# One-hots of a product-key gate build: token-by-token layout in place of lane-by-lane

## The chip, the cores and the metric

The kernel runs on one core of one Trainium2 chip. The metric is the device time of one execution in microseconds (us). The engines are named as in the profile: PE is TensorE (PEld its weight loads), DVE is VectorE, ACT is ScalarE, POOL is GpSimd, SP is SyncE, which only starts transfers here.

## The reference

One layer works on 256 tokens of width 2048: a retention group beside a gated recurrent group, then cross-attention to 256 memory tokens, then the part that matters here, a feed-forward of 16384 single-neuron experts (PEER):

```python
vals, ids = lax.top_k(sub_scores, 16)                    # 8 heads, two halves of 128 keys
cand = vals[:, :, 0, :, None] + vals[:, :, 1, None, :]
top_sc, pos = lax.top_k(cand.reshape(t, 8, 256), 16)     # 16 experts a head, 128 a token
eid = (i1 * 128 + i2).reshape(t, 128)
gate = jax.nn.softmax(top_sc, axis=-1).reshape(t, 128)
...
act = jax.nn.gelu(jnp.einsum('td,tkd->tk', xb, u_tab[eid]))
out = jnp.einsum('tk,tkd->td', gate * act, v_tab[eid])
```

A final RMSNorm follows. Everything is float32 at the interface.

## The kernel before

The 16384 experts are kept as 128 "rotated" rows of 128 lanes: a lane is a first index i1, and row r holds in lane i1 the expert whose second index is (r - i1) mod 128. The first 40 rows (`RD`) are computed densely, the other 88 (`RS`) only where tokens picked them: in each lane the 32 most used of them as dense columns as well, the rest by gathering single rows of U and V from HBM. The counts that decide this, and the gates of all rows, come out of the gate build.

A program order is written by hand as a main line of matmul blocks and a side line, `wv` (class `Weave`), a queue of generators. Each block of the main line calls `wv.pump(rate)`, which runs the side generators until their yields have used up that credit. The side code's instructions thus fall between those of the main line. Outside the stretches marked `manual_schedule`, the framework's planner may still change the order on each engine; data dependences are turned into semaphores by the framework.

The main line in the stretch at hand is `u_chunk` and `u_block` (L1173, L149): one column of U (128 experts) is two halves; each half is a load `raw<-in_U_dram` on SP's queue, a rounded copy `hi` on ACT (L135), the remainder `lo` on DVE (L136) and 24 matmuls (L156). The side line is `route`, which finds the 16 experts of each head, and then `gbuild` (L1116), which builds the gates.

`finish` (L830), called by `route` once for each half of 128 tokens, transposes the first index, the row number and the gate, so that a partition is a slot (8 heads times 16 picks) and a column is a token: `i1T`, `rT` in bfloat16, `gtT` in float32. It also fills a constant, `four` (L855): the numbers 0 to 127, each four times in a row, in bfloat16.

`gbuild` goes through the 256 tokens by four, 64 steps in all. A step does:

- two comparisons on DVE (L1132), which give `o2` (one-hot of the row number) and `c1` (one-hot of the first index), bfloat16, 128 partitions by 512 elements, laid out lane by lane: the four tokens of lane 0, the four of lane 1 and so on;
- a product on POOL (L1133): `og` is `o2` times the gate, float32, laid out token by token. It reads `o2` with a step of four elements;
- a copy on ACT (L1135): `o1` is `c1` in float32, token by token, read with the same step;
- one step later on PE: for each token a float32 product of `o1` and `og` (L1146) into the tile `G`, and a bfloat16 product of `c1` and the last 88 lanes of `o2` (L1149) that adds up counts in `cnt`. Both of its operands are read with a step of four elements;
- two copies on ACT (L1152, L1153) of `G` into the tiles `gs`.

The four arrays stand in rings of three (`n % 3`) within the tiles `kept`. Every eighth step ACT's queue issues three writes of `gs` to HBM (L1156, L1158, L1159, to `gd` and `gt`), and DVE multiplies two chunks of activations (L1164). When the counts are complete, `choose` (L956) picks the dense columns; `look_up` (L992), `compact` and the gathers (L1455, L1231) follow, and the main line goes on with U and then V.

Of the kernel before, what the change touches and what calls it, by code (L numbers as in the profile page):

```python
# [11 lines left out]
BF16 = mybir.dt.bfloat16  # L12
# [3 lines left out]
ALU = mybir.AluOpType  # L16
AX = mybir.AxisListType

P = 128
# [24 lines left out]
RD = 40  # L44
RS = P - RD
# [42 lines left out]
def hybrid_layer_kernel(ctx: ExitStack, tc: tile.TileContext, a: dict, out: bass.AP, dbg=None):  # L88
    nc = tc.nc
    V, A, G, PE = nc.vector, nc.scalar, nc.gpsimd, nc.tensor  # L90
# [28 lines left out]
    def sm(name):  # L119
        return ps2_.tile([P, 512], F32, tag="sm", name=name)  # L120

    ident = cp.tile([P, P], F32, name="ident")
    iota = cp.tile([P, P], F32, name="iota")
# [369 lines left out]
    for i in range(3):  # L493
        t = slot("qs" if i == 0 else "ms", [P, TT, 1024], "qkv"[i])
# [318 lines left out]
    i1T, rT, gtT, key, work, sel, sel2, idx = ({} for _ in range(8))  # L813
    flag = cp.tile([P, TT], F32, name="flag")

    def route():
# [11 lines left out]
        v4 = vals.rearrange("p (h c) j -> p h c j", c=2)  # L828
        i4 = idf.rearrange("p (h c) j -> p h c j", c=2)
        def finish(tt):  # L830
            four = gx["b"][:, 1536:1792].bitcast(BF16).rearrange("p (a b) -> p a b", b=4)
            gs = r3[:, 5, 0, :8]
            V.tensor_reduce(gs, gt, axis=AX.X, op=ALU.add)
            V.reciprocal(gs, gs)
            V.tensor_tensor(gt, gt, gs[:, :, None].to_broadcast([P, 8, 16]), op=ALU.mult)
            while "pb" not in done:
                yield 3.0
            i1, i2 = (ii[:, c].rearrange("p h j -> p (h j)") for c in range(2))
            rr = pgt.tile([P, P], F32, tag="rr", name="rr")
            tmp = tp.tile([P, P], F32, tag="gj", name="gj")  # L840
            V.tensor_tensor(rr, i1, i2, op=ALU.add)
            V.tensor_scalar(tmp, rr, float(P), -float(P), op0=ALU.is_ge, op1=ALU.mult)
            V.tensor_tensor(rr, rr, tmp, op=ALU.add)
            for _ in range(3):
                yield 2.0
            pt = sm("rT")
            for j, src in enumerate((i1, rr, gt.rearrange("p h j -> p (h j)"))):
                PE.transpose(pt[:, j * P:(j + 1) * P], src, ident)
            trio = gx["d"][:, 1536 + 256 * tt:1792 + 256 * tt]
            both = trio[:, :P].bitcast(BF16).rearrange("p (a b) -> p a b", a=2)  # L850
            A.copy(both, pt[:, :2 * P].rearrange("p (a b) -> p a b", a=2))
            A.copy(trio[:, P:], pt[:, 2 * P:3 * P])
            i1T[tt], rT[tt], gtT[tt] = both[:, 0], both[:, 1], trio[:, P:]
            if tt == 0:
                V.tensor_copy(four, iota[:, :, None].to_broadcast([P, P, 4]))  # L855
            nc.sync.dma_start(i1d[tt], both[:, 0])
            ri, rw = bits[tt], tmp
            V.tensor_copy(ri.bitcast(I32), rr)
            V.tensor_scalar(rw.bitcast(U32), ri, 3, None, op0=ALU.logical_shift_right)
            V.tensor_scalar(ri, ri, 7, None, op0=ALU.bitwise_and)  # L860
            V.tensor_copy(rw, rw.bitcast(I32))
            yield 1.0
            V.tensor_tensor(which[tt], iota[:, None, NCH:NCH + NW].to_broadcast([P, P, NW]),
                            rw[:, :, None].to_broadcast([P, P, NW]), op=ALU.is_equal)
            yield 1.3
            key[tt] = pgt.tile([P, P], F32, tag=f"key{tt}", name="key")
            work[tt] = pgt.tile([P, P], F32, tag=f"work{tt}", name="work")
            if tt == 0:
                jb = gx["b"][:, 1792:1920]
                V.tensor_scalar(tmp, iota, 1.0, None, op0=ALU.add)  # L870
                V.tensor_copy(jb.bitcast(I32), tmp)
                V.tensor_scalar(jb.bitcast(U32), jb.bitcast(U32), 23, None, op0=ALU.logical_shift_left)
                box["jb"] = jb
            V.tensor_scalar(rr, rr, float(P), -float(RD * P), op0=ALU.mult, op1=ALU.add)
            V.tensor_tensor(rr, rr, i1, op=ALU.add)
            V.tensor_copy(rr.bitcast(I32), rr)
            e, lead = rr.bitcast(U32), key[tt].bitcast(U32)
            gb, tu = gt.rearrange("p h j -> p (h j)").bitcast(U32), tmp.bitcast(U32)
            V.tensor_scalar(lead, e, 31, 31, op0=ALU.logical_shift_right, op1=ALU.logical_shift_left)
            V.tensor_tensor(lead, lead, box["jb"].bitcast(U32), op=ALU.bitwise_or)  # L880
            yield 1.5
            V.tensor_scalar(tu, gb, LOW, None, op0=ALU.bitwise_and)
            V.tensor_tensor(work[tt].bitcast(U32), tu, lead, op=ALU.bitwise_or)
            V.tensor_scalar(tu, e, 7, 1 << 20, op0=ALU.logical_shift_left, op1=ALU.bitwise_and)
            V.tensor_tensor(work[tt].bitcast(U32), work[tt].bitcast(U32), tu, op=ALU.bitwise_or)
            V.tensor_scalar(tu, gb, 20, 13, op0=ALU.logical_shift_right, op1=ALU.logical_shift_left)
            V.tensor_tensor(lead, lead, tu, op=ALU.bitwise_or)
            V.tensor_scalar(e, e, ROW, None, op0=ALU.bitwise_and)
            V.tensor_tensor(lead, lead, e, op=ALU.bitwise_or)
            yield 2.0  # L890
# [219 lines left out]
    acts, held_in, gx, bits, which, cnt = ({} for _ in range(6))  # L1110
# [5 lines left out]
    def gbuild():  # L1116
        prev = None
        cnt["t"] = pcn.tile([P, 512], F32, tag="cnt", name="cnt")
        rows = gt_.rearrange("(r p) t -> p r t", p=P)
        for n in range(T // 4 + 1):  # L1120
            nxt = None
            tt, t0 = divmod(4 * n, P)
            ss = slice(t0, t0 + 4)
            if n < T // 4:
                h0, q0 = n % 3 * 512, n % 3 * 256
                four = gx["b"][:, 1536:1792].bitcast(BF16).rearrange("p (a b) -> p a b", b=4)
                o1 = gx["a"][:, h0:h0 + 512].rearrange("p (a b) -> p a b", a=4)
                c1, o2 = (gx["d"][:, k + q0:k + q0 + 256].bitcast(BF16).rearrange("p (a b) -> p a b", b=4)
                          for k in (0, 768))
                og = gx["b"][:, h0:h0 + 512].rearrange("p (a b) -> p a b", a=4)  # L1130
                for o, ix in ((o2, rT), (c1, i1T)):
                    V.tensor_tensor(o, four, ix[tt][:, None, ss].to_broadcast([P, P, 4]), op=ALU.is_equal)  # L1132
                G.tensor_tensor(og, o2.rearrange("p a b -> p b a"), gtT[tt][:, ss, None].to_broadcast([P, 4, P]),  # L1133
                                op=ALU.mult)
                A.copy(o1, c1.rearrange("p a b -> p b a"))  # L1135
                nxt = (o1, o2, og, c1)
                yield 1.3
            if prev:
                o1, o2, og, c1 = prev
                m = n - 1  # L1140
                k = m % (GT // 4)
                if k == 0:
                    ga, gb = (slot(tag, [P, P // 2, GT], "gs") for tag in ("qs", "ms"))
                pt = sm("G")
                for j in range(4):
                    PE.matmul(pt.rearrange("p (c t) -> p c t", t=4)[:, :, j], o1[:, j], og[:, j],  # L1146
                              start=True, stop=True)
                for j in range(4):
                    PE.matmul(cnt["t"][:, :RS], c1[:, :, j], o2[:, RD:, j], start=(m == 0 and j == 0),  # L1149
                              stop=(m == T // 4 - 1 and j == 3))  # L1150
                ks = slice(4 * k, 4 * k + 4)
                A.copy(ga[:, :, ks], pt[:, :T].rearrange("p (c t) -> p c t", t=4))  # L1152
                A.copy(gb[:, :, ks], pt[:, T:].rearrange("p (c t) -> p c t", t=4))  # L1153
                if k == GT // 4 - 1:
                    ts = slice(4 * m + 4 - GT, 4 * m + 4)
                    A.dma_start(gd[:, :, m // (GT // 4)].rearrange("q p c t -> p q c t"),  # L1156
                                ga[:, 8 * ND:RD].rearrange("p (q c) t -> p q c t", c=8))
                    A.dma_start(rows[:, :P // 2 - RD, ts], ga[:, RD:])  # L1158
                    A.dma_start(rows[:, P // 2 - RD:, ts], gb)  # L1159
                    for i in range(ND):  # L1160
                        while f"u{i}" not in done:
                            yield 3.0
                        av = acts[i][:, :, ts]
                        V.tensor_tensor(av, ga[:, 8 * i:8 * i + 8], av, op=ALU.mult)  # L1164
                        yield 0.3
                yield 0.3
            prev = nxt
        done.add("gbuild")
# [717 lines left out]
```

## Time and profile before

| What | Value |
|---|---|
| Runs shown: median (lowest to highest) | 1977.03 us (1976.32 to 1978.99), 3 runs |
| Profiled execution, its own time | 1978.82 us |
| Its span, first to last instruction | 1977.0 us |
| Mean granted TensorE clock | 0.982 |
| Busy share of the span | PE 96%, PEld 80%, DVE 76%, ACT 43%, POOL 26% |
| First and last start of L1132 | 971.5 us and 1156.6 us |
| L1132, DVE, 128 instructions | 63.1 us busy |
| L1133, POOL, 64 instructions | 72.0 us busy |
| L1135, ACT, 64 instructions | 43.4 us busy |
| L1149, PE, 256 matmuls | 29.3 us busy |

Times in the views are microseconds from the start of the span, durations in group rows nanoseconds where they say "mean ns" or "duration ns". In a row of the timeline the first number is the start, the second the length, "x3" means that three instructions are merged, and the bracket gives the idle time before them and what ended it. The chain is followed back from the last instruction: at each step to what released it, or to its engine's instruction before.

### The profile page before, as it was taken

The page shows a single profiled execution, that of the slowest core. Times are in us where ns is not written, and L with a number is a line of the kernel's source. Part 1 is how long each engine was busy: PE and PEld are TensorE (multiplying, and loading weights), DVE is VectorE, ACT ScalarE, POOL GpSimd, SP SyncE. Part 2 cuts the span into 40 slices and gives each one's busy share as a digit, 9 for nine tenths or more (in the row PEclk, how much of TensorE's full clock was granted, in tenths as well). Part 3 has the DMA queues.
Part 4 walks back from the last instruction along what each step waited for, and adds up shares of the span by engine and source line. Part 5 has one row for each costly group of instructions (what it writes and reads, how often), then busy time and mean ns, then how long its engine had stood idle before and what let it go on. Part 6 is the DMA issues. An engine that isn't in the chain of part 4 may idle for free.

```text
span 1977.0 us, 28501 instructions
## 1 busy us (share of the span) xinstructions
PE 1896.1 (96%) x10644; PEld 1589.4 (80%) x10644; DVE 1500.9 (76%) x2304; ACT 851.6 (43%) x1324; POOL 517.7 (26%) x370
## 2 busy tenths in 40 slices
PE   9999999999999999999999887999989989999997
PEld 8888888888889888899899877988978668656563
DVE  6867968654566656899986667798879889687857
ACT  6566444544455554554456542333334343121111
POOL 0200010000000000000025421355443578477723
PEclk9999999999999999999999988999989999999999
DMA  8775755566664456755557888699898989999993
GB/s 297 260 224 170 208 195 182 154 185 195 185 185 156 149 167 217 251 176 164 186 179 142 166 258 277 235 395 362 321 383 318 383 315 399 379 387 372 421 411 125
DMA packets 203391, 500.97 MB, mean 253 GB/s; under 512 B 106777, under 2 KB 113049, under 8 KB 174873
## 3 DMA queue, kind: packets, MB, share of 16 engines
q1 hardware_dynamic: 72576, 256.33, 39.7%
q0 software_dynamic: 36096, 227.24, 29.5%
q10 hardware_dynamic: 94576, 15.54, 4.8%
q8 instruction: 84, 1.38, 0.3%
q14 instruction: 59, 0.48, 0.1%
HBM read 504.29 MB, written 21.30 MB: 266 GB/s over the span
## 4 chain that ended last, share of the span: by engine, by line
PE 56%; DMA 17%; DVE 14%; issue 9%; POOL 2%; ACT 2%; ACTq 0%; SPq 0%; POOLq 0%; DVEq 0%
PE wb L145 8%; PE xc L198 7%; PE xc L199 7%; PE xc L201 7%; DMA at<-in_Us_dram,idx 6%; PE acc L1213 6%; PE wb L147 4%; PE U L156 4%; DVE lo L136 4%; DMA gt<-gs 3%; DMA at<-in_Vs_dram,idx 2%; DMA kept<-in_V_dram 2%; PE G L1146 2%; PE acc L1194 2%; PE acc L1191 2%
## 5 line engine op out<-in xcount | busy, mean ns | idle before, releaser
L136 DVE TENSOR_TENSOR lo<-raw,hi 128x1024 fp32r<-128x1024 f32 x364 | 448.9, 1235 | 217.3 <-PE xc L201 125.7
L135 ACT CAST hi<-raw 128x1024 fp32r<-128x1024 f32 x364 | 382.1, 1053 | 352.4 <-PE xc L199 173.4
L156 PE MATMUL U<-xn,hi 128*128 128x256 f32 x1280 | 179.9, 292 | 3.8 <-ACT hi L135 3.8
L156 PEld LDWEIGHTS U<-xn,hi 128*128 128x128 f32 x1280 | 167.0, 199 | 4.7 <-ACT hi L135 4.7
L1462 DVE SCALAR_TENSOR_TENSOR junk<-at,h 128x2048 bf16<-128x2048 f32 x64 | 146.2, 2284 | 9.1 <-DMA at<-in_Us_dram,idx 8.9
L1470 DVE SCALAR_TENSOR_TENSOR hh<-at,coef,hh 128x2048 f32<-128x2048 f32 x46 | 108.0, 2348 | 47.3 <-DMA at<-in_Vs_dram,idx 46.7
L145 PE MATMUL U<-xn,hi 128*128 128x512 f32 x512 | 140.2, 407 | 0.0
L794 POOL DMA_DIRECT2D hn<-h x2 | 1.1, 565 | 510.4 <-DVE h L792 510.4
L1383 ACT CAST hi<-kept 128x1024 fp32r<-128x1024 f32 x52 | 53.6, 1051 | 186.9 <-DMA kept<-in_Vs_dram,dyn 127.0
L1455 POOL DMA_INDIRECT at<-in_Us_dram,idx x72 | 86.3, 1199 | 143.4 <-DVE junk L1462 114.4
L145 PE MATMUL wb<-hT,hi 128*128 128x512 f32 x448 | 116.9, 396 | 0.7 <-ACT hi L135 0.7
L1213 PE MATMUL acc<-kept,kept 128*128 128x512 f32 x256 | 110.2, 592 | 0.0
L1133 POOL TENSOR_TENSOR kept<-kept 128x512 f32<-128x512 bf16 x64 | 72.0, 1133 | 130.1 <-DVE kept L1132 90.2
L145 PEld LDWEIGHTS U<-xn,hi 128*128 128x128 f32 x512 | 92.9, 192 | 15.4
L156 PE MATMUL U<-xn,lo 128*128 128x256 f32 x640 | 96.0, 295 | 5.9 <-DVE lo L136 5.5
L1213 PEld LDWEIGHTS acc<-kept,kept 128*128 128x128 f32 x256 | 48.6, 190 | 60.4 <-issue 60.3
L156 PEld LDWEIGHTS U<-xn,lo 128*128 128x128 f32 x640 | 86.5, 201 | 9.2 <-DVE lo L136 8.9
L145 PEld LDWEIGHTS wb<-hT,hi 128*128 128x128 f32 x448 | 80.6, 189 | 14.8 <-ACT hi L135 0.9
L1400 DVE TENSOR_TENSOR lo<-uT,hi 128x512 fp32r<-128x512 f32 x128 | 81.8, 682 | 11.6 <-ACT hi L1381 8.7
L145 PE MATMUL wb<-xT,hi 128*128 128x512 f32 x352 | 90.1, 398 | 0.0
L1132 DVE TENSOR_TENSOR kept<-kept,kept 128x512 bf16<-128x512 bf16 x128 | 63.1, 543 | 32.8 <-PE cnt L1149 23.3
L1455 POOL DMA_INDIRECT at<-in_Vs_dram,idx x46 | 76.0, 1653 | 41.0 <-issue 18.6
(502 smaller groups left out, 4399.3 us busy)
## 6 DMA issues: line engine op xcount, KB each, us to landing
raw<-in_U_dram SPq DMA_DIRECT2D x80, 512.0 KB
raw<-in_w_qkv_dram SPq DMA_DIRECT2D x48, 512.0 KB
raw<-in_w_xyg_dram SPq DMA_DIRECT2D x44, 512.0 KB
raw<-in_V_dram SPq DMA_DIRECT2D x44, 512.0 KB
raw<-in_w_xk_dram SPq DMA_DIRECT2D x32, 512.0 KB
raw<-in_w_xv_dram SPq DMA_DIRECT2D x32, 512.0 KB
raw<-in_w_out_dram SPq DMA_DIRECT2D x32, 512.0 KB
raw<-in_w_xq_dram SPq DMA_DIRECT2D x32, 512.0 KB
```

What stands on the lines that cost most here:

```text
L135: A.copy(hi, raw)
L136: V.tensor_tensor(lo, raw, hi.bitcast(F32), op=ALU.subtract)
L145: PE.matmul(pt, hi[:, ks], xt[:, kb, :], start=(kb == 0), stop=(kb == KB - 1))
L156: PE.matmul(pt[:, :T], (lo if part == 2 else hi)[:, k * P:(k + 1) * P], x, start=(part == 0 and kb == 0), stop=(part == 2 and kb == KB - 1))
L198: PE.matmul(pt, xh, hi[:, w], start=(n == 0 and k == 0), stop=False)
L199: PE.matmul(pt, xl, hi[:, w], start=False, stop=False)
L201: PE.matmul(pt, xh, lo[:, w], start=False, stop=(n == 7 and k == 1))
L1213: PE.matmul(acc[dc][tt], av[:, c, tt * P:(tt + 1) * P], row[:, dc * 512:(dc + 1) * 512], start=False, stop=False)
L1400: V.tensor_tensor(los[t][:, s], pts[t][n], his[t][:, s].bitcast(F32), op=ALU.subtract)
L1455: G.indirect_dma_start(dst, None, src, bass.IndirectOffsetOnAxis(ap=ix, axis=0), bounds_check=n - 1, oob_is_err=False)
L1462: V.scalar_tensor_tensor(junk, gat, 1.0, h[0] if rows is None else rows, op0=ALU.mult, op1=ALU.mult, accum_out=coef[tt][:, k:k + 1])
L1470: V.scalar_tensor_tensor(hh[tt], gat, coef[tt][:, k:k + 1], hh[tt], op0=ALU.mult, op1=ALU.add)
```

## The change

The two one-hots are laid out token by token: 128 lanes of the first token side by side, then 128 of the second, and so on. The constant becomes `lanes`, 0 to 127 once, and a comparison now reads it four times over, against the index of a token repeated across 128 lanes. POOL's product and ACT's copy read straight rows, and so do both operands of the count's matmuls. What is written (`og`, `o1`), the sizes, the number of instructions, the yields and the rings stay as they were.

```diff
@@ finish
-            four = gx["b"][:, 1536:1792].bitcast(BF16).rearrange("p (a b) -> p a b", b=4)
+            lanes = gx["b"][:, 1536:1600].bitcast(BF16)
...
             if tt == 0:
-                V.tensor_copy(four, iota[:, :, None].to_broadcast([P, P, 4]))
+                V.tensor_copy(lanes, iota)
@@ gbuild
-                four = gx["b"][:, 1536:1792].bitcast(BF16).rearrange("p (a b) -> p a b", b=4)
+                lanes = gx["b"][:, 1536:1600].bitcast(BF16)
                 o1 = gx["a"][:, h0:h0 + 512].rearrange("p (a b) -> p a b", a=4)
-                c1, o2 = (gx["d"][:, k + q0:k + q0 + 256].bitcast(BF16).rearrange("p (a b) -> p a b", b=4)
+                c1, o2 = (gx["d"][:, k + q0:k + q0 + 256].bitcast(BF16).rearrange("p (a b) -> p a b", a=4)
                           for k in (0, 768))
                 og = gx["b"][:, h0:h0 + 512].rearrange("p (a b) -> p a b", a=4)
                 for o, ix in ((o2, rT), (c1, i1T)):
-                    V.tensor_tensor(o, four, ix[tt][:, None, ss].to_broadcast([P, P, 4]), op=ALU.is_equal)
-                G.tensor_tensor(og, o2.rearrange("p a b -> p b a"), gtT[tt][:, ss, None].to_broadcast([P, 4, P]),
+                    V.tensor_tensor(o, lanes[:, None, :].to_broadcast([P, 4, P]),
+                                    ix[tt][:, ss, None].to_broadcast([P, 4, P]), op=ALU.is_equal)
+                G.tensor_tensor(og, o2, gtT[tt][:, ss, None].to_broadcast([P, 4, P]),
                                 op=ALU.mult)
-                A.copy(o1, c1.rearrange("p a b -> p b a"))
+                A.copy(o1, c1)
...
-                    PE.matmul(cnt["t"][:, :RS], c1[:, :, j], o2[:, RD:, j], start=(m == 0 and j == 0),
+                    PE.matmul(cnt["t"][:, :RS], c1[:, j], o2[:, j, RD:], start=(m == 0 and j == 0),
                               stop=(m == T // 4 - 1 and j == 3))
```

## The prediction

> **What bounds the kernel now.** I read the page first, then a table of stretches around the gate build, the group rows and single lines there, the chain through one of its cycles, and the timeline of DVE and POOL beside it. The stretches:
>
> ```profile
> span 1977.0 us, 28501 instructions
> core 0: us, PE busy (x) PEld busy (x) DVE busy (x) ACT busy (x) POOL busy (x), PEclk, DMA share, GB/s
> 971.00:992.50 21.50, 19.47 (x155) 18.46 (x153) 21.43 (x38) 11.63 (x15) 3.38 (x3) 1.00 0.53 156
> 1018.00:1046.00 28.00, 28.00 (x255) 27.95 (x255) 19.46 (x32) 14.43 (x33) 11.71 (x10) 1.00 0.58 139
> 1066.00:1161.00 95.00, 83.97 (x720) 81.91 (x719) 62.80 (x106) 58.08 (x137) 42.09 (x40) 0.95 0.82 166
> 1213.00:1256.00 43.00, 39.01 (x303) 38.21 (x303) 27.03 (x109) 13.82 (x22) 1.23 (x2) 0.94 0.48 182
> ```
>
> DVE is full from 971 to 992.5, where routing still runs. Then PE is full, and from 1066 to 1161 nothing is: PE lacks 11 us of 95, DVE 32 us. What the gate build costs is decided there by hand-overs, not by one engine's load.
>
> The two views of DVE and POOL's lines (minimum, median and maximum of one instruction, then group rows with means):
>
> ```profile
> L1132 DVE TENSOR_TENSOR kept<-kept,kept x128: 401/413/1284, 971.5 to 1156.6; 128x512 bf16<-128x512 bf16 x128
> L1133 POOL TENSOR_TENSOR kept<-kept x64: 1035/1154/2035, 972.1 to 1162.0; 128x512 f32<-128x512 bf16 x64
> L1164 DVE TENSOR_TENSOR kept<-gs,kept x16: 409/416/1269, 1034.2 to 1169.8; 128x256 f32<-128x256 f32 x16
> ...
> L916 DVE TENSOR_TENSOR eq<-rt,iota 128x2048 bf16<-128x2048 bf16 x2 | 4.6, 2288 | 0.0
> L919 DVE TENSOR_TENSOR eq<-eq,rt 128x2048 bf16<-128x2048 bf16 x2 | 2.4, 1218 | 0.0
> ```
>
> A comparison of 512 elements takes 413 ns, the same as L1164 with 256 elements of float32. So it moves two elements in the time of one. But its maximum is three times its median, and the next view says why. DVE and POOL in one cycle of eight steps:
>
> ```profile
> 1095.32 1.23 DVE L136 TENSOR_TENSOR lo<-raw,hi 128x1024 fp32r<-128x1024 f32 x1 [1.51 <-ACT hi L135]
> 1098.48 3.06 POOL L1133 TENSOR_TENSOR kept<-kept 128x512 f32<-128x512 bf16 x3 [6.63 <-PE G L1146]
> 1101.51 0.76 DVE L1132 TENSOR_TENSOR kept<-kept,kept 128x512 bf16<-128x512 bf16 x2 [4.97 <-PE cnt L1149]
> 1102.01 1.17 POOL L1133 TENSOR_TENSOR kept<-kept 128x512 f32<-128x512 bf16 x1 [0.48 <-DVE kept L1132]
> 1102.76 1.04 DVE L1132 TENSOR_TENSOR kept<-kept,kept 128x512 bf16<-128x512 bf16 x2 [0.49 <-PE cnt L1149]
> 1103.54 1.16 POOL L1133 TENSOR_TENSOR kept<-kept 128x512 f32<-128x512 bf16 x1 [0.36 <-DVE kept L1132]
> 1104.01 1.31 DVE L1132 TENSOR_TENSOR kept<-kept,kept 128x512 bf16<-128x512 bf16 x2 [0.21 <-PE cnt L1149]
> 1105.06 1.17 POOL L1133 TENSOR_TENSOR kept<-kept 128x512 f32<-128x512 bf16 x1 [0.36 <-DVE kept L1132]
> 1105.24 2.08 DVE L136 TENSOR_TENSOR lo<-raw,hi 128x1024 fp32r<-128x1024 f32 x1
> 1109.09 3.96 DVE L1132 TENSOR_TENSOR kept<-kept,kept 128x512 bf16<-128x512 bf16 x9
> ```
>
> The remainder L136 takes 1.23 us at 1095, with POOL idle, and 2.08 us at 1105.24, where POOL's product runs until 1106.23. A pair of comparisons takes 0.76 us undisturbed, and 1.04 or 1.31 when it starts inside a product. Products started by themselves go 1.02 us apart (three in 3.06); with comparisons between they start 1.53 apart (1102.01, 1103.54). So these DVE instructions and POOL's product exclude each other, and a step costs their sum. The chain at the same place:
>
> ```profile
> 1101.08 0.33 PE cnt L1149 x4
> 1101.40 0.93 PE G L1146 x8
> ...
> 1105.24 0.73 DVE lo L136
> ...
> 1107.24 0.41 DVE kept L1132
> 1107.65 1.51 DVE kept L1164 x2
> 1109.17 0.35 DVE kept L1132
> ...
> 1109.56 0.50 PE cnt L1149 x4
> ```
>
> From 1101.08 back it is PE's; from 1104 to 1109.56 it is DVE's queue: comparisons, a remainder, L1164 twice, and the comparison that PE's count waits for. The cycle comes five times between 1066 and 1161.
>
> **The change part by part.** *The comparisons (L1132).* Their second source is now one index repeated 128 times in a row, instead of four neighbours. From L1164 (median 416 ns, 256 elements) to L916 (2288 ns, 2048), one element at a time costs 1.045 ns, so 512 cost 0.68 us; two at a time is today's 0.413. L916 has such a repeated source and L919, as large, has rows of neighbours: 2288 against 1218. But L916 also reads float32, so it doesn't settle it. Ends: +0 and +0.27 us each; I take +0.27, as the row with the repeated source is the nearer. The Trainium skill, Vector Engine (DVE) Microarchitecture Reference, section 5.1, reports a single element read again and again by a two-source instruction at the one-per-cycle rate, and a row read again and again at two; by that rule the sum is the one below, without it the first rival. No run here shows it.
>
> *Before 992.5* six comparisons lie in a full DVE: 6 x 0.27 = +1.6. The constant shrinks from 512 to 128 elements:
>
> ```profile
> L855 DVE CAST kept<-iota x1: 429/429/429, 952.6 to 952.6; 128x512 bf16<-128x512 f32 x1
> ```
>
> It saves between 0 and 0.43 us; I take 0.2. **Term A: +1.4 us.**
>
> *From 1020 to 1038* PE takes a step in 1.25 us (G and count) and POOL in 1.5:
>
> ```profile
> 1021.74 1.17 POOL L1133 TENSOR_TENSOR kept<-kept 128x512 f32<-128x512 bf16 x1 [41.36 <-DVE kept L1132]
> 1032.49 1.19 POOL L1133 TENSOR_TENSOR kept<-kept 128x512 f32<-128x512 bf16 x1 [0.46 <-DVE kept L1132]
> ...
> 1034.02 0.93 PE G L1146 x8
> 1035.27 2.91 PE U L156 x24
> ```
>
> Three steps were ready before; the product at 1032.49 is the tenth, done at 1033.68, and PE uses it at 1034.02: 0.3 us to spare. Seven steps at +0.53 (two comparisons) bring it to 1037.4, so PE is 3.4 late; four counts behind it give back 0.7 (below). **Term B: +2.7**, between 0 and +3.7.
>
> *From 1046 to 1066* ACT's queue carries the chain (copies and the issue of the writes), DVE beside it:
>
> ```profile
> 1049.61 3.81 DVE L1132 TENSOR_TENSOR kept<-kept,kept 128x512 bf16<-128x512 bf16 x6 [7.57 <-POOL kept L1133]
> 1054.87 3.02 DVE L1132 TENSOR_TENSOR kept<-kept,kept 128x512 bf16<-128x512 bf16 x6
> 1058.56 1.61 DVE L1132 TENSOR_TENSOR kept<-kept,kept 128x512 bf16<-128x512 bf16 x2 [0.67 <-ACT kept L1135]
> ```
>
> Fourteen comparisons make 3.7 us against 0.67 of idle time. Ends 0 and 3.7; ACT waits for `c1` in part only. **Term C: +2.5.**
>
> *The five cycles.* From the count's end at 1101.41: three steps at 1.53 become 2.06, +1.6; the remainder behind them is as late; then the comparison at 1107.24 and the one at 1109.17, +0.27 each: PE's count starts 2.1 us later, and its next one, a pair further on, another 0.3. The nine comparisons at 1109.09 grow by 2.1 us, but after them DVE idles (1.51 and 4.97 in the rows above): hidden. PE's part gets shorter by the counts: three groups before DVE's part, 0.17 each, -0.5. Net +1.9; **Term D: 5 x 1.9 = +9.5.** Ends: 0, if the planner lets the comparisons run ahead into DVE's 32 idle us, and 16 x 0.27 = 4.3 a cycle, +21.5.
>
> *The counts (L1149).* A group of four takes 0.33 us on the chain, 82 ns a matmul with its weight load. The nearest straight bfloat16 row, with 128 weights but 11 columns for 88, takes 27.5 ns:
>
> ```profile
> 1178.52 1.76 PE L1001 MATMUL look<-words,kept 128*128 128x11 bf16 x64
> ```
>
> Ends 27.5 and 82; I take 40, nearer the straight row: -0.17 a group. Where PE waits for DVE that is worth nothing, so it is counted in B and D alone. The Trainium skill speaks against this gain: SBUF — State Buffer, section "Door 1: The DMA port swizzle", has lines of 16 bytes of which two hits hide the access, so a step of four bfloat16 would be free. By that rule B and D lose 0.7 and 2.5, and the time would be 3 us more; the distance of 82 to 27.5 speaks for the gain.
>
> *POOL's product* keeps its number and size; only the step of its source goes. I take it unchanged (1.04 us), since no row has a straight bfloat16 source on POOL. *ACT's copy*, *G*, the transfers: nothing; ACT's copies can only get shorter, and outside 1046 to 1066 ACT waits for DVE or PE. *The last steps* (two comparisons at 1156): **term E, +0.5.**
>
> *Does it reach the end?* What follows the last step:
>
> ```profile
> 1166.18 33.13 DMA gt<-gs
> ...
> 1255.62 0.99 POOL L1231 DMA_INDIRECT row<-in_Us_dram,dyn  x1 [41.77 <-PE uT L1372]
> ```
>
> The last write starts with the last step, a load of indices waits for it, and from 1213 to 1256 PE is on U columns (39 of 43 us) that stand behind the gate build in its queue. Nothing there waits for anything independent of it, so I pass the delay on one to one.
>
> Sum: 1.4 + 2.7 + 2.5 + 9.5 + 0.5 = +16.6 us on the profiled execution's 1978.8, so 1995.4. That execution is 1.8 us above the median of the runs (1977.0), which gives **1994 us**.
>
> **The rivals.** *Faster:* the comparisons stay at 413 ns, DVE taking the repeated index in pairs. Then only the counts change. For: L1132 is two-byte throughout, unlike L916. Against: L916 against L919. Half of the 256 x 42 ns lies on the chain, as PE waits for DVE in the rest: -6, 1971 us. It decides as soon as a comparison grows by less than about 0.08 us (6 us over the some 75 that lie on the chain).
>
> *No change:* the longer comparisons are hidden, because the planner orders them earlier; DVE has the room (32 idle us of 95, and some 80 comparisons there need 22). Against: in the rows above the comparisons wait for the count that frees their ring slot, which order can't change. Term D goes; the other terms make 7.1, the counts give back up to 6: +1, 1978 us.
>
> *All of it on the path:* DVE and POOL together become the bound for the whole build, 128 x 0.27 = +34: 2011 us. For: the mutual exclusion. Against: the idle stretch at 1095 to 1101 in every cycle.
>
> *POOL gets faster* with a straight source: at most to the length of a product of half as many bytes. A third off its 1.04 us takes 0.35 of the 0.53 out of each step, so two thirds of B and D: about 1986 us, still slower.
>
> **How the numbers follow.** This measurement can tell 0.2% from no change, about 4 us. Chances: the forecast with its variants on counts and POOL, 1985 to 2004 us, 0.66; all on the path 0.12; hidden 0.10; comparisons unchanged 0.12. So slower 0.78, same 0.10, faster 0.12. The range, 1973 to 2010 us, takes in the hidden case and nearly all of the full path, and leaves out the faster rival and the far tail, under 0.2.
>
> **What would show it.** After the change: L1132's median near 0.68 us (0.41: first rival); products 2.05 us apart between comparisons instead of 1.53, and near 1.04 long; a count group of 0.16 us on the chain; PE's waits for L1132 at the counts longer than today's 10 us (row below); the last product starting near 1179 us instead of 1162; the stretch from there to the end as long as now. The prediction is wrong if the last product is late and the end isn't, or if the order of comparisons and products differs from today's.
>
> ```profile
> PE cnt L1149 <- DVE kept L1132: 10.0, 6, 1.8
> ```

## The result, and the profile after

| | Kernel before | Changed kernel |
|---|---|---|
| Median of 4 runs (lowest to highest) | 1976.67 us (1973.88 to 1978.99) | 1995.66 us (1994.11 to 2000.39) |
| Profiled execution, span | 1977.0 us | 1998.6 us |

The change makes the kernel slower: the ratio of the times is 1.010, 95% interval 1.008 to 1.012, 19.0 us between the medians. The forecast was 1994 us.

The changed kernel has one line more inside the comparison, so everything below moves by one: POOL's product is L1134, ACT's copy L1136, the gate products L1147, the counts L1150, the transposition at which the sparse phase starts L1373. The single lines of the changed kernel, minimum, median and maximum in nanoseconds, then first and last start:

```profile
span 1998.6 us, 28509 instructions
L1132 DVE TENSOR_TENSOR kept<-kept,kept x128: 660/679/1582, 969.1 to 1166.6; 128x512 bf16<-128x512 bf16 x128
L855 DVE CAST kept<-iota x1: 209/209/209, 950.2 to 950.2; 128x128 bf16<-128x128 f32 x1
L1134 POOL TENSOR_TENSOR kept<-kept x64: 1031/1420/16137, 970.0 to 1175.4; 128x512 f32<-128x512 bf16 x64
L1150 PE MATMUL cnt<-kept x256: 202/205/297, 1017.9 to 1170.7; 128*128 128x88 bf16 x128
PE cnt L1150 <- DVE kept L1132: 21.4, 18, 2.4
```

A comparison takes 679 ns where it took 413. POOL's product is no shorter where nothing disturbs it: 1031 ns at least, against 1035 before. The counts' matmuls end sooner, and PE waits at them for the comparison for 21.4 us instead of 10.0. POOL's timeline in the first burst, the same stretch in which the products stood 1.5 us apart before:

```profile
1019.13 1.42 POOL L1134 TENSOR_TENSOR kept<-kept 128x512 f32<-128x512 bf16 x1 [23.03 <-DVE kept L1132]
1021.18 1.42 POOL L1134 TENSOR_TENSOR kept<-kept 128x512 f32<-128x512 bf16 x1 [0.63 <-DVE kept L1132]
1023.23 1.42 POOL L1134 TENSOR_TENSOR kept<-kept 128x512 f32<-128x512 bf16 x1 [0.63 <-DVE kept L1132]
```

The spacing is 2.05 us. A product between comparisons takes 1.42 us instead of 1.17; I read the 0.4 us above the undisturbed 1.03 as time in which the product, already started, waits for DVE's second comparison. DVE's timeline beside it and the table of the later stretch show who is full now:

```profile
1018.37 9.48 DVE L1132 TENSOR_TENSOR kept<-kept,kept 128x512 bf16<-128x512 bf16 x10
...
core 0: us, PE busy (x) PEld busy (x) DVE busy (x) ACT busy (x) POOL busy (x), PEclk, DMA share, GB/s
1064.00:1170.00 106.00, 85.42 (x714) 80.44 (x715) 95.89 (x104) 56.99 (x141) 54.06 (x41) 0.90 0.65 138
```

Ten comparisons run end to end in 9.48 us, without a gap, held up by the products between them (6.10 us where the product is left out, below). In the cycles DVE is busy for 95.9 us of 106 (62.8 of 95 before), part of it waiting for POOL inside its instructions, as the longest comparison of 1.58 us shows. From 1018 us to the last write's issue the comparisons' share of the chain goes from 3.1% to 23.9%, that of PE's U columns from 24.6% to 7.1%; that of the gate products only from 23.4% to 19.4%. So the alternation of DVE and POOL now sets the pace of the build for much of the time, and PE for the rest.

### The profile page after: what moved, and what is told of

Read it like the earlier page. It is cut to its first block, busy times and chain, and to the rows that moved or that the text cites. A ratio compares the mean times of both kernels' runs of the same rounds, so it can differ in the third digit from the quotient of the medians.

```text
span 1998.6 us, 28509 instructions
## 1 busy us (share of the span) xinstructions
PE 1896.4 (95%) x10644; PEld 1585.1 (79%) x10644; DVE 1550.1 (78%) x2304; ACT 849.4 (42%) x1324; POOL 548.9 (27%) x370
## 4 chain that ended last, share of the span: by engine, by line
PE 54%; DMA 16%; DVE 15%; issue 11%; POOL 2%; ACT 1%; DVEq 0%; POOLq 0%; ACTq 0%; SPq 0%
PE wb L145 8%; DMA at<-in_Us_dram,idx 7%; PE xc L198 7%; PE xc L199 7%; PE xc L201 7%; PE acc L1214 5%; PE wb L147 4%; DVE lo L136 4%; PE U L156 4%; DMA kept<-in_V_dram 3%; DVE kept L1132 2%; DMA at<-in_Vs_dram,idx 2%; PE G L1147 2%; DMA gt<-gs 1%; DVE hh L1471 1%
## 5 line engine op out<-in xcount | busy, mean ns | idle before, releaser
L1134 POOL TENSOR_TENSOR kept<-kept 128x512 f32<-128x512 bf16 x64 | 101.4, 1593 | 116.5 <-DVE kept L1132 81.3
L1132 DVE TENSOR_TENSOR kept<-kept,kept 128x512 bf16<-128x512 bf16 x128 | 114.3, 954 | 12.6 <-PE cnt L1150 7.0
L1456 POOL DMA_INDIRECT at<-in_Vs_dram,idx x46 | 80.7, 1755 | 46.4 <-DVE hh L1471 20.4
L145 PE MATMUL wb<-xT,hi 128*128 128x512 f32 x352 | 89.1, 393 | 0.5 <-ACT hi L135 0.5
```

The lines of the kernel that those rows point to most:

```text
L145: PE.matmul(pt, hi[:, ks], xt[:, kb, :], start=(kb == 0), stop=(kb == KB - 1))
L1132: V.tensor_tensor(o, lanes[:, None, :].to_broadcast([P, 4, P]), ix[tt][:, ss, None].to_broadcast([P, 4, P]), op=ALU.is_equal)
L1456: G.indirect_dma_start(dst, None, src, bass.IndirectOffsetOnAxis(ap=ix, axis=0), bounds_check=n - 1, oob_is_err=False)
```

## The experiments

The times of the kernel before differ a little from one set of runs to the next (1976.3 to 1978.4 us), so each ratio is against the runs of the kernel before on the same chip. A and B are the theories of the first four expectations; C, that the planner's other order makes the loss, came from comparing the queues of the two kernels, which do differ.

**Both one-hots token by token, each index stored twice.** The changed kernel with a copy of the indices in which each one stands twice in a row; a comparison then reads runs of two.

```diff
+            twice = gx["a"][:, 1536 + 256 * tt:1792 + 256 * tt].bitcast(BF16).rearrange("p (a t b) -> p a t b", a=2, b=2)
+            A.copy(twice, pt[:, :2 * P].rearrange("p (a t) -> p a t", a=2)[:, :, :, None].to_broadcast([P, 2, P, 2]))
...
-                                    ix[tt][:, ss, None].to_broadcast([P, 4, P]), op=ALU.is_equal)
+                                    ix[tt][:, ss, None, :].to_broadcast([P, 4, P // 2, 2]), op=ALU.is_equal)
```

> The changed layout, with each token's index stored twice in a row, so that a comparison reads neighbours again. Theory A (the comparisons got longer because the repeated index made them run one element at a time, and that is the whole loss): a comparison takes 0.41 us again, a count group stays at 0.16 us, products between comparisons are 1.53 us apart again, and the time is 1971 to 1976 us, under the kernel before by what the shorter counts give. Theory B (the loss comes from the layout in another way, the planner's other order or the later hand-overs): comparisons shorten, but the time stays at 1985 us or more.

Measured: 1969.71 us against 1978.44, ratio 0.9967 (0.9952 to 0.9981). Its comparison and its counts:

```profile
L1135 DVE TENSOR_TENSOR kept<-kept,kept x128: 398/414/1261, 967.3 to 1143.9; 128x512 bf16<-128x512 bf16 x128
L1154 PE MATMUL cnt<-kept x256: 202/205/213, 1015.7 to 1144.5; 128*128 128x88 bf16 x128
```

The comparison is at 414 ns again, products between comparisons start 1.51 us apart again (1016.68 and 1018.19 us), the counts keep the short time, and the kernel beats both others, by 0.33% the one before (1.3 us better than A's range). The layout itself does no harm; the repeated index did. B falls.

**The old layout with long comparisons.** The kernel before with its constant in float32 (in another tile, for its size), nothing else.

```diff
-                four = gx["b"][:, 1536:1792].bitcast(BF16).rearrange("p (a b) -> p a b", b=4)
+                four = gx["a"][:, 1536:2048].rearrange("p (a b) -> p a b", b=4)
```

> The kernel before, lane by lane, with its constant kept in float32, so that the comparisons cannot run in pairs; nothing else of the change. Theory A: a comparison takes 0.68 us, the count group stays at 0.33 us, and the time is that of the changed kernel plus the counts' gain it lacks, 1996 to 2000 us. Theory B: longer comparisons alone are mostly hidden in DVE's idle time, 1985 us or less.

Measured: 2000.67 us, ratio 1.0108 (1.0091 to 1.0125).

```profile
L1132 DVE TENSOR_TENSOR kept<-kept,kept x128: 666/680/1547, 969.5 to 1166.8; 128x512 bf16<-128x512 f32 x128
L1149 PE MATMUL cnt<-kept x256: 240/261/281, 1018.5 to 1171.5; 128*128 128x88 bf16 x128
```

With 680 ns a comparison and the counts as they were, the whole loss is there (0.7 us above A's range). So longer comparisons make the loss in the old layout too; the new one isn't needed for it.

**One of the two one-hots token by token.** First the one of the first index, `c1`:

```diff
+                V.tensor_tensor(c1, lanes[:, None, :].to_broadcast([P, 4, P]),
+                                i1T[tt][:, ss, None].to_broadcast([P, 4, P]), op=ALU.is_equal)
...
-                    PE.matmul(cnt["t"][:, :RS], c1[:, :, j], o2[:, RD:, j], start=(m == 0 and j == 0),
+                    PE.matmul(cnt["t"][:, :RS], c1[:, j], o2[:, RD:, j], start=(m == 0 and j == 0),
```

> The kernel before with the one-hot of the first index alone laid out token by token: 64 comparisons of 0.68 us, 64 of 0.41, straight weights for the counts, their moving rows still with a step of four. Theory A: about half of the loss, 1984 to 1989 us; products 1.79 us apart between comparisons. Whether the counts' weight load or the moving rows set their 82 ns: near 40 ns if the weights did, near 82 if the rows did. Theory B: no such proportion, under 1981 or over 1992 us.

Then the one of the row number, `o2`, in the same manner (`c1[:, :, j], o2[:, j, RD:]`):

> The kernel before with the one-hot of the row number alone laid out token by token: 64 comparisons of 0.68 us, straight moving rows for the counts and a straight source for POOL, weights still with a step of four. Theory A: about half of the loss, 1984 to 1990 us, a little above the sister with the other one-hot, since POOL waits for this one and starts later. Counts near 40 ns if the moving rows set their 82 ns, near 82 if the weights did. Theory B: no such proportion, under 1981 or over 1992 us.

Measured: 1986.97 us, ratio 1.0040 (1.0024 to 1.0056), and 1985.51 us, ratio 1.0041 (1.0025 to 1.0056): 8.5 and 7.1 us, by the medians, somewhat under half of the loss each and within A's ranges. The counts with `c1` straight:

```profile
L1153 PE MATMUL cnt<-kept x256: 238/258/297, 1018.2 to 1160.1; 128*128 128x88 bf16 x128
```

And with `o2` straight:

```profile
L1153 PE MATMUL cnt<-kept x256: 202/205/297, 1019.1 to 1160.3; 128*128 128x88 bf16 x128
```

Straight weights leave a count at 258 ns (261 before), straight moving rows bring it to 205, as in the full change. What shortens the counts is the moving side, but for 3 ns. The kernel with the shorter counts is 1.5 us ahead of its sister by the medians and not at all by the ratios, so they are worth little while PE waits for DVE. The expected order (`o2` slower, as POOL waits for it) did not appear.

Where the time goes in these two is worth a look. The first and last start of the gate products, and the first transposition of the sparse phase, with `c1` straight:

```profile
L1150 PE MATMUL G<-kept,kept x512: 272/275/471, 1017.3 to 1162.3; 128*128 128x128 f32 x171
L1376 PE MATMUL uT<-ident,row x352: 271/273/444, 1260.5 to 1501.1; 128*128 128x128 f32 x176
```

The build takes 145.0 us, as before the change (144.6), but from its first product to the first transposition it is 243.2 us instead of 233.7 (rows further down): between the first and the last gate product PE runs 338 matmuls of U columns instead of 370, and behind the last one 480 instead of 448. The build kept its length because U columns moved behind it, and the delay shows there.

**The two kernels in the written order.** Both with the U columns and the build inside `manual_schedule`, which makes their queues the same, instruction for instruction.

```diff
-    for i in range(early):
-        u_chunk(i)
+    with tc.manual_schedule(engines=ENGINES):
+        for i in range(early):
+            u_chunk(i)
...
```

The kernel before:

> The kernel before, with the stretch of the dense U columns and the gate build in the order in which it is written, without the planner. Its twin is the changed kernel in the same written order: instruction for instruction the same queues on every engine. This one is the twin's yardstick; its own time may lie anywhere from 1970 to 2010 us, since the planner's moves are missing.

The changed kernel:

> The changed kernel in the written order, as its twin. Theory A (longer comparisons on the chip, DVE and POOL excluding each other): slower than the twin by 12 to 25 us, as with the planner. Theory C (the planner, which lays the two kernels out in different orders, makes most of the 19 us): within 6 us of the twin.

Measured: 2175.13 us (ratio 1.1019, 1.0976 to 1.1061) and 2197.22 us (1.1116, 1.1076 to 1.1156), 22.1 us apart. The yardstick is far slower than I had allowed, so the planner's moves are worth some 200 us here; but the change costs in the written order about what it costs with the planner, as A expected. C falls as the main cause; how much the planner's other order adds or saves in the first pair isn't shown. The products' spacing and the build's length, first in the kernel before, then in the changed one:

```profile
1162.91 1.16 POOL L1133 TENSOR_TENSOR kept<-kept 128x512 f32<-128x512 bf16 x1 [6.71 <-DVE kept L1132]
1164.43 1.15 POOL L1133 TENSOR_TENSOR kept<-kept 128x512 f32<-128x512 bf16 x1 [0.36 <-DVE kept L1132]
...
L1146 PE MATMUL G<-kept,kept x512: 272/275/553, 1117.7 to 1307.4; 128*128 128x128 f32 x171
```

```profile
1159.27 1.42 POOL L1134 TENSOR_TENSOR kept<-kept 128x512 f32<-128x512 bf16 x1 [0.63 <-DVE kept L1132]
1161.31 1.42 POOL L1134 TENSOR_TENSOR kept<-kept 128x512 f32<-128x512 bf16 x1 [0.62 <-DVE kept L1132]
...
L1147 PE MATMUL G<-kept,kept x512: 272/275/561, 1121.1 to 1333.1; 128*128 128x128 f32 x171
```

From 1.52 to 2.04 us a step, and from 189.7 to 212.0 us for the build: 22.3 us. The two profiled executions differ by 29.8 us in span (2169.6 and 2199.4 us), more than the medians: 3.4 us before the first gate product and some 4 behind the last come on top.

**Both kernels without POOL's product.** The instruction is taken out, and its output is set to zero once.

```diff
+        G.memset(gx["b"][:, :1536], 0.0)
...
-                G.tensor_tensor(og, o2, gtT[tt][:, ss, None].to_broadcast([P, 4, P]),
-                                op=ALU.mult)
```

The kernel before:

> The kernel before without POOL's product: the gated one-hots are zeros written once, so the dense gates come out as zero; counts, picks and gathers stay. Theory A with the exclusion as its price: PE's waits in the gate build fall, 1960 to 1972 us. Without an exclusion POOL's absence would change little: 1974 us or more.

The changed kernel:

> The changed kernel without POOL's product, dense gates zero as in its twin. If the exclusion makes the longer comparisons dear, DVE alone now holds two comparisons of 0.68 us a step, 1.28 us, about PE's pace: within 6 us of the twin. If the length of the comparisons is enough by itself: 12 us or more above the twin.

Measured: 1972.35 us (ratio 0.9972, 0.9954 to 0.9989) and 1968.38 us (0.9948, 0.9926 to 0.9970). The comparisons of the kernel before without the product:

```profile
L1133 DVE TENSOR_TENSOR kept<-kept,kept x128: 394/419/428, 969.7 to 1145.5; 128x512 bf16<-128x512 bf16 x128
```

And of the changed one:

```profile
L1133 DVE TENSOR_TENSOR kept<-kept,kept x128: 660/684/696, 969.6 to 1134.3; 128x512 bf16<-128x512 bf16 x128
```

Two things are to be seen. The maxima, 1284 and 1582 ns with the product, are down to 428 and 696: what stretched single comparisons was POOL's product and nothing else. And with comparisons of 684 ns the changed kernel is no longer the slower one: 4.0 us under its twin, though the two intervals overlap. The ten comparisons of the first burst show where the time went; they took 9.48 us with the product:

```profile
1017.82 6.10 DVE L1133 TENSOR_TENSOR kept<-kept,kept 128x512 bf16<-128x512 bf16 x10
```

So the comparisons' length costs time mainly through the exclusion. Not all of it need be: the shorter counts are in the 4.0 us too, and in the first experiment they were in a gain of 8.7 us, so longer comparisons may cost some 5 us without the product as well, where with it the changed kernel and that of the first experiment are some 26 us apart. What POOL's product costs the kernel before by itself is small, 4.8 us; the first number is 0.4 us over its expected range. And the removal takes PE's waits for `og` away as well, so the two kernels don't show the exclusion alone.

**One one-hot token by token, its index stored twice.** What makes the gain of the first experiment? `o2` alone, then `c1` alone, comparisons at 0.41 us in both.

```diff
+                V.tensor_tensor(o2.rearrange("p a (u b) -> p a u b", b=2),
+                                lanes.rearrange("p (u b) -> p u b", b=2)[:, None].to_broadcast([P, 4, P // 2, 2]),
+                                twos[tt][:, ss, None, :].to_broadcast([P, 4, P // 2, 2]), op=ALU.is_equal)
```

> The kernel before with the one-hot of the row number alone laid out token by token, its index stored twice in a row so that its comparison stays at 0.41 us. The counts' moving rows and POOL's source become straight, the counts' weights and ACT's source keep their step. If the shorter counts (39 ns a matmul, as in the run with this one-hot alone) make the gain of the kernel with both in pairs: 1968 to 1973 us. If ACT's shorter copies make it: 1975 to 1979 us.

> The kernel before with the one-hot of the first index alone laid out token by token, its index stored twice. The counts' weights and ACT's source become straight, the moving rows keep their step, so counts stay at 81 ns a matmul and ACT's copy takes 0.62 instead of 0.69 us. If the counts make the gain: 1975 to 1979 us. If ACT's copies make it: 1968 to 1973 us.

Measured: 1969.80 us (ratio 0.9968, 0.9953 to 0.9982) and 1975.92 us (0.9988, 0.9976 to 0.9999). Counts and ACT's copies with `o2`:

```profile
L1157 PE MATMUL cnt<-kept x256: 202/205/233, 1021.0 to 1150.2; 128*128 128x88 bf16 x128
L1143 ACT CAST kept<-kept x64: 655/692/818, 972.9 to 1151.0; 128x512 f32<-128x512 bf16 x64
```

With `c1`:

```profile
L1157 PE MATMUL cnt<-kept x256: 238/258/263, 1017.9 to 1151.5; 128*128 128x88 bf16 x128
L1143 ACT CAST kept<-kept x64: 618/632/738, 969.8 to 1152.1; 128x512 f32<-128x512 bf16 x64
```

The gain goes with the counts, 6.5 us here, and hardly with ACT's copies (0.4 us); both times lie in the ranges expected for that case. The kernel with `o2` has a straight source for POOL too, but its product is no shorter by it, 1032 ns at least against 1035 before. `o2` alone with its index stored twice is as fast as both, and copies half as many indices, though it needs both constants.

## Why the prediction was right

The forecast came 1.7 us under the median, and its likeliest case is what happened. Step by step, by the profiled executions. The kernel before: first the rows with the first and last start of the gate products and of the transpositions, then a row of the chain (start, length, engine, line and count), the eleventh step's gate product:

```profile
L1146 PE MATMUL G<-kept,kept x512: 270/275/422, 1019.7 to 1164.3; 128*128 128x128 f32 x171
L1372 PE MATMUL uT<-ident,row x352: 270/273/329, 1253.4 to 1493.7; 128*128 128x128 f32 x176
```

```profile
1045.57 0.89 PE G L1146 x8
```

The same of the changed kernel (in the chain the eleventh step is merged with the two behind it; a group of counts and the last write stand below it):

```profile
L1147 PE MATMUL G<-kept,kept x512: 271/275/582, 1017.0 to 1178.9; 128*128 128x128 f32 x171
L1373 PE MATMUL uT<-ident,row x352: 270/273/472, 1270.4 to 1513.3; 128*128 128x128 f32 x176
```

```profile
1045.78 2.75 PE G L1147 x24
...
1107.65 0.33 PE cnt L1150 x8
...
1180.84 14.35 DMA gt<-gs
```

The waits for POOL's product (sum in us, number, longest), before and after:

```profile
PEld G L1146 <- POOL kept L1133: 4.3, 2, 3.3
PE G L1146 <- POOL kept L1133: 3.1, 1, 3.1
```

```profile
PEld G L1147 <- POOL kept L1134: 8.9, 9, 4.2
PE G L1147 <- POOL kept L1134: 5.6, 6, 4.0
```

| Step | Predicted | Measured | How |
|---|---|---|---|
| Comparison | 0.68 us | 0.679 us | rows above |
| Spacing of products | 2.06 us | 2.05 us | timeline |
| Group of four counts | 0.16 us | 0.165 us | chain at 1107.65, half of 0.33 |
| Product undisturbed, copy of the constant | 1.04 us, 0.2 us saved | 1.03 us, 0.22 us saved | rows above |
| A, constant to first gate product | +1.4 us | -0.3 us | 67.1 to 66.8 us |
| B, to the eleventh step | +2.7 us | +2.9 us | 25.9 to 28.8 us |
| C, D and E, to the last | +12.5 us | +14.4 us | 118.7 to 133.1 us |
| To the first transposition | 0 | +2.4 us | 89.1 to 91.5 us |
| To the end of the span | 0 | +4.6 us | 723.6 to 728.2 us |

The mechanism stood as told: DVE leaves the mode in which it moves two elements at a time, comparisons and product exclude each other, and the step grows from 1.53 to 2.05 us. The sum of the three lengths that the prediction spoke of is too large, though: 1.04 and twice 0.413 make 1.87 us, 1.03 and twice 0.679 make 2.39. The step was a third of a microsecond shorter in both kernels, and what it grew by, 0.52 us, is what the two comparisons grew by, 0.53.

*Term A* failed. By the timeline the six comparisons together went from 3.11 to 4.56 us, by 1.45 where 1.6 was forecast. But two other two-source instructions, L901 and L910, which POOL's products had held up, were held up no longer (one remainder lost 0.5 us in their place), and the planner put one L922 (0.69 us) behind the remainder on which the U columns ahead of the gate products start. Before, then after:

```profile
972.63 1.00 DVE L901 TENSOR_TENSOR cand<-rt 128x256 f32<-128x256 f32 x1
979.57 0.95 DVE L910 TENSOR_TENSOR rt<-rt 128x128 f32<-128x128 f32 x1
991.18 1.22 DVE L136 TENSOR_TENSOR lo<-raw,hi 128x1024 fp32r<-128x1024 f32 x1
```

```profile
969.99 0.39 DVE L901 TENSOR_TENSOR cand<-rt 128x256 f32<-128x256 f32 x1
977.47 0.27 DVE L910 TENSOR_TENSOR rt<-rt 128x128 f32<-128x128 f32 x1
988.42 1.21 DVE L136 TENSOR_TENSOR lo<-raw,hi 128x1024 fp32r<-128x1024 f32 x1
```

From the constant to this remainder it is 38.6 us before and 38.2 after. DVE was full here, as the prediction had it; what it had wrong is that all else in DVE's queue would stay as it was.

*C, D and E* were 1.9 us too small together, although 27 matmuls of U columns had left the build. The rows are of U columns between the first and the last gate product, before and after: the stretch, its length, then the busy time and number of PE's matmuls and of its weight loads, the granted clock and the DMA's share and rate.

```profile
1019.70:1164.30 144.60, 54.95 (x370) 50.32 (x369) 0.96 0.76 160
```

```profile
1017.00:1178.90 161.90, 51.96 (x343) 46.01 (x342) 0.92 0.64 142
```

I had walked the cycles with today's order, but the planner laid DVE's queue out otherwise; the prediction had named that as a sign of being wrong. So the cost is confirmed as a whole, and by the written-order pair without a change of order, but not cycle by cycle. PE's waits at the counts doubled (10.0 to 21.4 us); its waits for `og` grew from 3.1 to 5.6 us, those of its weight loads from 4.3 to 8.9. That A to E make 17.0 us where 16.6 were forecast is partly luck: A is too large, C to E are too small.

The other signs came out by halves. The last product of POOL starts at 1175.4 us, not near 1179, and the stretch from there to the end is 823.2 us instead of 815.0, not as long as before. From the last gate product on, the steps came out 7.0 us longer instead of equal. The first 2.4 belong to the build: PE runs 475 matmuls of U columns there instead of 448. Those U columns in PE's queue pass the delay on; the last write, which the prediction named beside them, does not, since it lands at 1195.2 us, 4.1 us earlier than before (1166.18 and 33.13 make 1199.3). The other 4.6 I don't explain: the stretch from the first transposition to the end is 723.6 us before, 728.2 after, and 721 to 731 in the ten experiments, the longest in the changed kernel without a product, whose build is the shortest. The changed kernel's profiled execution was also the slowest of its four; the 2.4 us by which it was ahead when the constant was filled are as unexplained. The sum of all of it, -2.4 - 0.3 + 2.9 + 14.4 + 2.4 + 4.6, is the 21.6 us between the spans; between the medians it is 19.0.

Of the rivals, *faster* was near in its price and wrong in its condition: with comparisons left at 414 ns the kernel gains 8.7 us, where 6 had been written (half of 256 times 42 ns is 5.4); DVE took pairs from runs of two, not from one repeated element. The Trainium skill has both (Vector Engine (DVE) Microarchitecture Reference, section 5.1): one element read again and again by a two-source instruction runs at one per cycle, and two-byte operands run at two per cycle where the innermost row has a step of one and more than one element. The 679 and 414 ns here agree with it. *No change* fell with the 19.0 us. *POOL gets faster* fell: 1031 against 1035 ns. *All on the path*, 34 us, would have needed a chain without idle stretches; DVE still idles for 5.7 us in one of the cycles, until PE's gate product is through.

On the counts the page and the chip differ. The Trainium skill's rule of the 16-byte lines (SBUF — State Buffer, section "Door 1: The DMA port swizzle") makes a step of four bfloat16 free. For TensorE's moving rows it is not: 258 to 261 ns a matmul against 205, by the medians. The measurement decides; for the weights, the same step cost 3 ns at most (261 against 258 with the moving rows in steps, 205 either way with straight ones).

## What to carry to other kernels

When a layout is turned for the sake of its readers, price first what the writer loses: here one index repeated along the row took DVE out of the mode in which it moves two 16-bit elements at a time, and storing each index twice gave it back and kept the readers' gain. Where DVE's two-source instructions and POOL's work alternate within a ring, add up both engines' times per step and compare the sum with PE's step: before the change neither engine looked full, yet together they set the pace in the bursts (here a third of a microsecond under the plain sum). Of several readers of a strided operand, find the one that pays; here only the moving rows of the counts did, as ACT's copies got shorter to no effect.

## What the runs showed of the hardware that was not expected

A product on POOL can be starved for long by DVE. In the changed kernel one took 16.1 us (in the first experiment's 17.6); POOL's and DVE's timelines:

```profile
979.96 16.14 POOL L1134 TENSOR_TENSOR kept<-kept 128x512 f32<-128x512 bf16 x1 [3.37 <-DVE kept L1132]
...
994.52 0.68 DVE L922 TENSOR_TENSOR eq<-eq 128x1024 bf16<-128x1024 bf16 x1
995.12 0.28 DVE L833 TENSOR_REDUCE rt<-rt 128x8 f32<-128x128 f32 x1
995.32 1.08 DVE L922 TENSOR_TENSOR eq<-eq 128x512 bf16<-128x512 bf16 x1
```

DVE ran two-source instructions back to back from 980 on; the product ended at 996.1, about its own length after the first instruction with a single source since then (a reduction at 995.12), which I read as letting it in, and the two-source instruction behind that one was held up in turn (1.08 us where its like takes 0.42). It cost nothing that shows, as the first gate product started only at 1017. And for a step of 8 bytes in its moving rows a matmul of 88 columns in bfloat16 takes some 55 ns longer by itself (205 to 261) and 41 ns longer in a row of its kind (groups of four in 0.33 us instead of 0.165); for the same step in its weights 3 ns at most.
